# The beginning of an RWKV-7 scan: the last columns of v between its first products, and the first inverse ahead of the second pair's scores

## The chip, the cores and the metric

The kernel runs on one core of one Trainium2 chip. The metric is the device time of one execution in microseconds. The time before is the median of three runs, 1482.53 us (1478.01 to 1484.24). One further execution was profiled; it took 1480.0 us, and its trace has a span of 1478.1 us. All instants below are microseconds from the start of that span. Engines are named as the profile does: PE is TensorE, DVE VectorE, ACT ScalarE, POOL GpSimd, SP SyncE (here it only issues transfers).

## The reference

Two layers over 1024 tokens of width 1024, each with a norm before and a residual add after, and a last norm. The first layer (chunked gMLP beside dilated attention) is not touched. The second is RWKV-7 time mixing. Its inputs are shifted mixes of the normed activations, its projections r, k, v and a gate g, and its core is a recurrence per head with a 64x64 state:

```python
xr, xw, xk, xv, xa, xg = [h + xx * mu[i] for i in range(6)]
r, k, v, g = xr @ w_r, xk @ w_k, xv @ w_v, xg @ w_g
...
def step(state, inp):
    r_t, w_t, k_t, v_t, kk_t, a_t = inp
    sa = jnp.einsum('bhvk,bhk->bhv', state, -kk_t)
    state = (state * w_t[:, :, None, :]
             + sa[..., None] * (kk_t * a_t)[:, :, None, :]
             + v_t[..., None] * k_t[:, :, None, :])
    y_t = jnp.einsum('bhvk,bhk->bhv', state, r_t)
    return state, y_t
...
y = (y + bonus) * jax.nn.silu(g)
return y @ w_o
```

## The kernel before, in words

**The scan.** The 1024 tokens are cut into 16 chunks of 64, for 16 heads. Inside a chunk the recurrence is a triangular system per head: with M, the strictly triangular products of the chunk's scaled keys (`A`, `BK`), the chunk needs X, the inverse of a unit triangular matrix built from M. Chunks are handled in pairs (b2); eight pairs in all. For one pair the work is:

- `ld`: SyncE loads `A` and `BK` (0.5 MB each) of a chunk from DRAM, where the projections left them (L1001, L1003).
- `al` (alphas): 64 small matmuls (L1043, L1046) into two PSUM banks; ScalarE copies them to `M` (L1047) and `AK` (L1048).
- `sM`, `lM`: M goes to DRAM in four stores (L1055) and comes back, in another layout, as `Nt` (L1099, two loads).
- `ip`: GpSimd clears the inverse's tiles. `ia`, `ie`, `ib` (8 pieces): the inverse itself, on VectorE alone (L1121 to L1164).
- `ic`, `lX`: the result goes to DRAM as `XT` (L1171) and comes back as `X` (L1179).
- `mx`, `ma`, `mb`: the merge, two small groups of matmuls (L1197, L1210) with a copy by ScalarE after each (L1200, L1213).
- `sc` (half of a chunk's scores, 32 matmuls, L1030, one PSUM bank, copied by ScalarE to `MY`), `mA`, `mY` (triangular masks, GpSimd), `dec` (BK times the decay, GpSimd, L1062), `T` (transposes of BK, L1072).
- Then the serial part per chunk: `V` (L1225), `W` (L1235), `U` (L1250), `st` (the state, L1275, added by VectorE, L1277), `Y`.

**The gate.** 16 column blocks of the gate's projection (first eight for tokens 0 to 511, then eight for 512 to 1023) are TensorE's filler between these small products. A piece `g1` is three matmuls of 128x512 (L943); eight pieces make a block, which ScalarE passes through SiLU (L949). Block n needs its weight: `L` loads it (SyncE, L928, 0.5 MB), `wx` splits it into a high part (ScalarE, L105) and a low part (L106; GpSimd for n from 2 to 7, VectorE for the others). `xl` loads the gate's operands of the second half of the tokens into the tiles of the first half (L937, 1 MB each). 64 pieces stand in the beginning.

**What sets the order.** Up to the scan a scheduler places the instructions. In the scan each engine, SyncE's queue too, runs its instructions in the order in which the code calls them. That order is three strings of such names with a number each: `SCAN_START`, `SCAN_STEP` (six times), `SCAN_END`. An instruction whose input is not there holds up all that stands behind it on its engine. Matmuls of the gate and of `V`, `W`, `U`, `st` share three PSUM banks, `al`, `T`, `ma` and `mb` two others, which are given out in turn.

**v.** The projection of v is made in four chunks of 256 columns, each for eight blocks of 128 tokens: 24 matmuls of 128x256 (L153) for a block and chunk, since every operand is split into a high and a low part and three of the four products are taken. Two blocks fill a PSUM bank; ScalarE copies it out (L855) and SyncE stores it (L857). After the first half of the last chunk the operands of the gate are made (`mixed`: L736, L739 on ScalarE, L737 and L740 on VectorE, L740 on GpSimd too), then the second half follows. All of v is done before `SCAN_START` begins.

Of the kernel before, what the change touches and what calls it, by code (L numbers as in the profile page):

```python
# [8 lines left out]
F32 = mybir.dt.float32  # L9
# [8 lines left out]
P = 128  # L18
KT = D // P
NB = S // P  # L20
CB = 256
# [28 lines left out]
EVEN_PLAN = (  # L50
    "q0 k0 h0 z2 h1 q1 h2 k1 h3 va0 s0 h4 u0 h5 z3 h6 z0 h7 va1 s1 u1 z1")
SCAN_START = (
# [4 lines left out]
SCAN_STEP = (  # L57
    "U0 al0 ib2 st0 al1 Y0 uv1 keep1 mA0 mA1 W1 sM0 sc0 ib3 ld6 U1 sc1 g1 mY0 mY1 ic0 st1 dec0 lM0 Y1 g1 W2 keep2 "
    "ip0 lX0 gx1 uv2 sc2 Yd0 T0 g1 sc3 ia0 ld7 mx0 ma0 dec1 ie0 g2 mb0 g2 T1 g2 ib3 gl2")
# [771 lines left out]
            nc.sync.dma_start(g.BK_d[64:128, f * 8:(f + 1) * 8, p, 1 - j], BK[64:128, :, j])  # L831


def odd_layer(g, a, hT, wt, out):
    nc, tc = g.nc, g.tc
    st = ExitStack()
# [13 lines left out]

    def ev_v(c):
        def fn(b2, ps):
            t = g.s2([P, 2, 2, CB // 2], F32, "rt")
            for j in range(2):
                nc.scalar.activation(t[:, j].rearrange("p e (q d) -> p e q d", d=CH),  # L855
                                     ps[:, j].rearrange("p (q e d) -> p e q d", e=2, d=CH), AF.Copy)
                nc.sync.dma_start(g.v_d[(2 * b2 + j) * P:(2 * b2 + j + 1) * P, :, c * P:(c + 1) * P], t[:, j])  # L857
        return fn
# [6 lines left out]
    w = load_wm(g, plan[0][1], 0)  # L865
# [4 lines left out]
    for j, (i, W, fn, ld, ev, c) in enumerate(plan):  # L870
        if c == 0:
            x, xn = xn, ({}, {})
        if j + 1 < len(plan):
            nxt = plan[j + 1][3](g, plan[j + 1][1], plan[j + 1][5] * CB)
        else:
            gate = Gate(g, a["rw_wg"][0], xn)
            gate.load(0)
            gate.load(1)
            gate.split(0)
            gate.split(1)  # L880
        if j == 9:
            norms(g)
        if j == XD:
            mixed_out(g, hT, 5, 1, g.xg_d)
        if c == 3:
            ni = plan[j + 1][0] if j + 1 < len(plan) else 5
            fn(g, x, w, ev(c), (0,))
            mixed(g, hT, ni, (0,), xn)
            fn(g, x, w, ev(c), (1,))
            if ni != 5:  # L890
                mixed(g, hT, ni, (1,), xn)
        else:
            fn(g, x, w, ev(c))
        w = nxt
# [83 lines left out]
class Rwkv:  # L978
# [326 lines left out]
    def start(self, gate):  # L1305
        g, nc = self.g, self.g.nc

        def zs(i):
            nc.gpsimd.memset(self.new_S(0), 0.0)

        self.pm = g.bB([P, 2, 2, 4, CH], "pm")
        ops = dict(L=gate.load, wx=gate.split, xl=gate.load_x, ld=self.load,
                   g=lambda i: [next(gate.rest, None) for _ in range(i)],
                   sc=lambda i: self.scores(i // 2, i % 2), al=self.alphas, sM=self.store_M, lM=self.load_M,
                   ip=self.inverse_p, ia=self.inverse_a, ie=self.inverse_d, ib=lambda i: [next(self.rows, None) for _ in range(i)],
                   ic=self.inverse_c, lX=self.load_X, mx=self.merge_x, ma=self.merge_a, mb=self.merge_b,
                   dec=self.decayed, T=self.transposed, mA=self.mask_AK, mY=self.mask_MY,
                   uv=self.load_uv, V=lambda i: list(self.Wkeys(i)), W=self.W, keep=self.keep, zs=zs)
        for name, i in order(SCAN_START):
            ops[name](i)  # L1320
# [244 lines left out]
```

## Time and profile before

| | us |
|---|---|
| median of three runs | 1482.53 (1478.01 to 1484.24) |
| profiled execution, its own time | 1480.0 |
| its span | 1478.1 |
| TensorE busy | 1308.3 (89%) |
| VectorE busy | 897.8 (61%) |
| ScalarE busy | 627.8 (42%) |
| GpSimd busy | 548.4 (37%) |
| last matmul of v ends, about | 1003.1 |
| first inverse on VectorE | 1038.1 to 1069.2 |
| first merge product (L1197), all but two of it | 1078.3 |
| first `U` (L1250) | 1089.0 |

Matmuls are pipelined, so a busy TensorE is not TensorE at its peak: 87 matmuls of v begin in 10 us, though each is shown as lasting 0.28 us. In the chain of waits a row gives start, duration and what ran; "SPq" is the time in which SyncE issues a transfer, "DMA a<-b" the time from the end of the issue to the transfer's end. In rows by stretch the columns are the stretch, its length, busy time (and instructions) of PE, weight loads, DVE, ACT and POOL, then the granted TensorE clock, the share of the DMA engines and GB/s. In rows by group the two numbers after the bar are busy us and mean ns of one, and behind the second bar stands the idle time before them and what ended it.

### The profile page before, as it was taken

Reading aid. Unit: us, or ns where it says so; the run is one execution under the profiler, and the core shown is the slowest. Engines: PE = TensorE matmul, PEld = TensorE weight load, DVE = VectorE, ACT = ScalarE, POOL = GpSimd, SP = SyncE. Lnnn points to the kernel's source line nnn. Section 1 sums busy time; section 2 is a strip of 40 time slices with the busy share of each in tenths; the row PEclk is TensorE's granted clock in tenths of the full one; section 3 lists DMA queues with packets and bytes.
Section 4 is the critical chain, followed back from the end, with each engine's and each line's share of the span. In section 5 each row is a group of like instructions: output and inputs, shape, how many; then the busy total and the mean of one; then the engine's idle time right before and its main releaser. Section 6 shows DMA issues by size and latency. Waiting matters only on the chain.

```text
span 1478.1 us, 30910 instructions
## 1 busy us (share of the span) xinstructions
PE 1308.3 (89%) x12773; PEld 1108.9 (75%) x12773; DVE 897.8 (61%) x1489; ACT 627.8 (42%) x1188; POOL 548.4 (37%) x353
## 2 busy tenths in 40 slices
PE   5899999899997999999997868998978788887877
PEld 5887788778896799978864436896767666667877
DVE  8741535663557426771599888512856677768884
ACT  4421535552454323552545554323434344454322
POOL 8750102030112612221343353203644444387751
PEclk9999999899999999999999979998978898979998
DMA  6377435350443334224177547517586666676412
GB/s 221 86 259 196 114 128 158 83 131 15 137 121 101 124 119 143 74 74 140 43 220 203 125 103 204 143 48 207 142 244 162 154 168 167 187 212 228 143 36 93
DMA packets 253275, 209.15 MB, mean 141 GB/s; under 512 B 79648, under 2 KB 215424, under 8 KB 253136
## 3 DMA queue, kind: packets, MB, share of 16 engines
q1 hardware_dynamic: 249536, 198.27, 47.1%
q10 hardware_dynamic: 3600, 8.91, 1.8%
q8 instruction: 100, 1.64, 0.5%
q14 instruction: 39, 0.32, 0.1%
HBM read 135.71 MB, written 71.43 MB: 140 GB/s over the span
## 4 chain that ended last, share of the span: by engine, by line
PE 53%; DVE 17%; DMA 9%; issue 8%; ACT 6%; POOL 4%; SPq 2%; ACTq 0%; DVEq 0%; POOLq 0%
PE pj L153 33%; PE pj L943 4%; PE pt L572 2%; PE pj L1477 2%; DMA kl<-dk 1%; DMA BK<-BK_d 1%; DMA w<-in_rw_a_dram 1%; DMA XT<-xm 1%; PE sp L562 1%; PE sp L559 1%; PE op L580 1%; DMA X<-XT 1%; ACT wh L105 1%; PE py L1285 1%; DVE xm L737 1%
## 5 line engine op out<-in xcount | busy, mean ns | idle before, releaser
L106 POOL TENSOR_TENSOR wl<-wraw,wh 128x1024 fp32r<-128x1024 f32 x38 | 93.6, 2466 | 168.6 <-ACT wh L105 157.5
L106 DVE TENSOR_TENSOR wl<-wraw,wh 128x1024 fp32r<-128x1024 f32 x46 | 70.8, 1545 | 94.5 <-ACT wh L105 51.4
L153 PE MATMUL pj<-hh,wh 128*128 128x512 f32 x320 | 127.3, 398 | 0.0
L153 PE MATMUL pj<-hh,wl 128*128 128x512 f32 x320 | 126.6, 396 | 0.0
L153 PE MATMUL pj<-hl,wh 128*128 128x512 f32 x320 | 126.6, 396 | 0.0
L105 ACT ACTIVATE wh<-wraw 128x1024 fp32r<-128x1024 f32 x84 | 88.1, 1056 | 61.9 <-DMA wraw<-in_w_in_even_dram 25.1
L153 PE MATMUL pj<-xl,wh 128*128 128x512 f32 x256 | 102.3, 400 | 2.6 <-DVE xl L740 2.6
L153 PE MATMUL pj<-xh,wh 128*128 128x512 f32 x256 | 102.2, 401 | 2.4 <-ACT ks L789 2.4
L153 PE MATMUL pj<-xh,wl 128*128 128x512 f32 x256 | 101.8, 398 | 0.2 <-POOL wl L106 0.2
L566 DVE CUSTOM_DVE_ANT_0 sc<-sp,tb 128x128 f32<-128x128 f32 (+3 forms) x64 | 48.2, 753 | 59.4 <-PE sp L562 50.8
L1477 PE MATMUL pj<-wh,yh 128*128 128x256 f32 x256 | 75.4, 294 | 5.1 <-DVE x L1481 3.9
L1477 PE MATMUL pj<-wh,yl 128*128 128x256 f32 x256 | 74.4, 291 | 4.6 <-POOL yl L106 4.5
L153 PE MATMUL pj<-wh,hh 128*128 128x256 f32 x256 | 75.1, 296 | 3.2 <-ACT hh L265 2.9
L737 DVE SCALAR_TENSOR_TENSOR xm<-hT,pr,xm 128x512 f32<-128x512 f32 x56 | 50.0, 933 | 44.0 <-ACT xm L736 43.7
L153 PE MATMUL pj<-wh,hl 128*128 128x256 f32 x256 | 75.3, 295 | 1.2 <-DVE hl L266 1.2
L153 PE MATMUL pj<-wh,yl 128*128 128x256 f32 x256 | 73.7, 288 | 1.9 <-POOL yl L624 1.9
L153 PE MATMUL pj<-wl,hh 128*128 128x256 f32 x256 | 74.6, 292 | 0.0
L153 PE MATMUL pj<-wh,yh 128*128 128x256 f32 x256 | 73.3, 286 | 0.8 <-ACT yh L623 0.8
L1477 PE MATMUL pj<-wl,yh 128*128 128x256 f32 x256 | 74.0, 289 | 0.0
L153 PE MATMUL pj<-wl,yh 128*128 128x256 f32 x256 | 72.9, 285 | 0.0
L153 PE MATMUL pj<-wh,xh 128*128 128x256 f32 x256 | 72.2, 282 | 0.6 <-ACT ks L789 0.5
L153 PE MATMUL pj<-wl,xh 128*128 128x256 f32 x256 | 72.2, 282 | 0.0
(320 smaller groups left out, 4062.3 us busy)
## 6 DMA issues: line engine op xcount, KB each, us to landing
wraw<-in_w_in_even_dram SPq DMA_DIRECT2D x28, 512.0 KB
tb<-tb SPq DMA_DIRECT2D x16, 512.0 KB
A_d<-AR SPq DMA_DIRECT2D x16, 512.0 KB
wraw<-in_rw_wg_dram SPq DMA_DIRECT2D x16, 512.0 KB
A<-A_d SPq DMA_DIRECT2D x16, 512.0 KB
BK<-BK_d SPq DMA_DIRECT2D x16, 512.0 KB
xt<-in_x_dram SPq DMA_DIRECT2D x8, 512.0 KB
dv<-vt SPq DMA_DIRECT2D x16, 256.0 KB
```

The costliest lines, as they stand in the source:

```text
L105: nc.scalar.activation(hi, raw, AF.Copy)
L106: sub.tensor_tensor(lo, raw, hi.bitcast(F32), OP.subtract)
L153: nc.tensor.matmul(ps, a(k), b(k), start=(n == 0), stop=(n == 3 * KT - 1))
L559: nc.tensor.matmul(sp[:, c0:c1], qs[:, b * P:(b + 1) * P], kh[:, c0:c1], start=True, stop=False)
L562: nc.tensor.matmul(sp[:, c0:c1], qs[:, b * P:(b + 1) * P], kl[:, c0:c1], start=False, stop=True)
L566: nc.vector.tensor_tensor_reduce(sc[:, :n], sp[:, :n], tb[:, off:off + n], 1.0, BIG, OP.add, OP.min, mn)
L572: nc.tensor.transpose(pt[:, j - j0, :], sc[:, j * P:(j + 1) * P], g.ident)
L580: nc.tensor.matmul(op[:, s0:QW], vt[:, j, :], pth[j // 4][:, j % 4, s0:QW], start=(j == 0), stop=False)
L737: nc.vector.scalar_tensor_tensor(t, hT[kk, f][:, j, 0:512], g.pr[:, i, k:k + 1], t, op0=OP.mult, op1=OP.add)
L943: nc.tensor.matmul(ps, u[:, k], v[:, k % 2], start=(k == 0 and i == 0), stop=(k == KT - 1 and i == 2))
L1285: nc.tensor.matmul(self.py[64 - 64 * e:128 - 64 * e, q], t["MY"][:, 8 * e + q], t["UV"][:, e, q], start=q == 0, stop=False)
L1477: nc.tensor.matmul(ps[:, i, :], u[:, k], v[:, k % 4], start=(k == 0 and j == 0), stop=(k == KT - 1 and j == 2))
```

## The change

The second half of v's last chunk is no longer made before the scan. It becomes a generator of eight steps of 12 matmuls each (half a block of 128 tokens), which a new name in the string, `vp`, advances: three before the first `al`, one between the two, four after the second. Its output tile is named `XT` instead of `rt`. The string `SCAN_START` is rewritten; it holds the same names and 64 pieces of the gate as before, and `vp` beside them. `SCAN_STEP` and `SCAN_END` are unchanged.

```diff
 SCAN_START = (
-    "g4 L2 g4 L4 L3 g7 al0 al1 sM0 ip0 wx2 g2 sc0 L7 g2 sc1 dec0 L9 uv0 ld2 g3 wx3 sc2 g2 wx4 sc3 dec1 g2 lM0 T0 "
-    "ld3 L6 g4 mA0 mY0 ia0 L5 g2 al2 wx5 g2 sc4 T1 ld4 g3 al3 sM1 ie0 sc5 dec2 g3 wx6 ib8 sc6 g2 sc7 dec3 uv1 T2 "
-    "zs0 g3 ic0 g4 wx7 mA1 mY1 ip1 lM1 lX0 keep0 g4 T3 g5 L8 mx0 xl0 V0 uv2 ma0 g2 wx8 xl1 ia1 mA2 g2 xl2 mb0 ie1 "
-    "W0 ld5 mA3 g2 xl3 ib3")
+    "vp3 al0 vp1 al1 sM0 ip0 vp2 lM0 vp2 ia0 ie0 g4 L2 sc0 g4 L4 L3 sc1 dec0 ib8 ld2 g7 wx2 g2 sc2 L7 g2 sc3 dec1 "
+    "L9 uv0 T0 ld3 g3 wx3 ic0 ip1 lX0 g2 wx4 T1 al2 mA0 mY0 g2 L6 ld4 g4 sc4 L5 g2 wx5 mx0 al3 sM1 V0 uv2 ma0 sc5 "
+    "dec2 g2 mb0 T2 g3 lM1 sc6 g3 wx6 sc7 dec3 ia1 mA1 mY1 uv1 g2 zs0 g3 ie1 T3 g4 wx7 keep0 g4 mA2 g5 L8 xl0 g2 "
+    "wx8 xl1 g2 xl2 W0 ld5 mA3 g2 xl3 ib3")
...
+def last_values(g, x, w, evac):
+
+    wh, wl = w
+    for b in range(4, 8):
+        sl = slice((b % 4) * P, (b % 4 + 1) * P)
+        if b % 2 == 0:
+            ps = g.bA([P, 2, CB], "pj")
+        n = 0
+        for k in range(KT):
+            for i, v in ((0, wh), (0, wl), (1, wh)):
+                g.nc.tensor.matmul(ps[:, b % 2, :], x[i][k // 2, 1][:, k % 2, sl], v(k), start=(n == 0), stop=(n == 3 * KT - 1))
+                n += 1
+            if k == 3:
+                yield
+        if b % 2:
+            evac(b // 2, ps)
+        yield
...
     def ev_v(c):
         def fn(b2, ps):
-            t = g.s2([P, 2, 2, CB // 2], F32, "rt")
+            t = g.s2([P, 512], F32, "XT").rearrange("p (j e c) -> p j e c", j=2, e=2)
...
             mixed(g, hT, ni, (0,), xn)
-            fn(g, x, w, ev(c), (1,))
             if ni != 5:
+                fn(g, x, w, ev(c), (1,))
                 mixed(g, hT, ni, (1,), xn)
+            else:
+                gate.last = last_values(g, x, w, ev(c))
...
-        ops = dict(L=gate.load, wx=gate.split, xl=gate.load_x, ld=self.load,
+        ops = dict(vp=lambda i: [next(gate.last, None) for _ in range(i)], L=gate.load, wx=gate.split, xl=gate.load_x, ld=self.load,
```

Two places where the order moves are of use later. In the new kernel the same statements have line numbers higher by up to 21, and instances of a tile carry other numbers. The first is SyncE's queue at the scan's first loads. `A_9328` and `A_9332` are the first two chunks' A before, `BK_9330` and `BK_9334` their BK, `wraw` a weight of the gate. Before:

```order
L857 DMA v_d_126<-rt_9260 256x1x128 x2
L1001 DMA A_9328<-A_d_116 128x1024
L1001 DMA A_9332<-A_d_116 128x1024
L928 DMA wraw_9352<-in_rw_wg_dram 128x8x128
L857 DMA v_d_126<-rt_9314 256x1x128 x2
L928 DMA wraw_9369<-in_rw_wg_dram 128x8x128
L928 DMA wraw_9371<-in_rw_wg_dram 128x8x128
L1003 DMA BK_9330<-BK_d_117 128x1024
L1003 DMA BK_9334<-BK_d_117 128x1024
L1055 DMA MA_0_129<-M_9395 32x16x32 x4
```

And now:

```order
L876 DMA v_d_126<-XT_9158 256x1x128 x2
L1022 DMA A_9220<-A_d_116 128x1024
L1022 DMA A_9224<-A_d_116 128x1024
L1024 DMA BK_9222<-BK_d_117 128x1024
L1024 DMA BK_9226<-BK_d_117 128x1024
L876 DMA v_d_126<-XT_9318 256x1x128 x2
L1076 DMA MA_0_129<-M_9268 32x16x32 x4
L1120 DMA Nt_9393<-MA_0_129 64x1024 x2
L876 DMA v_d_126<-XT_9420 256x1x128 x2
```

BK follows A at once, and `Nt` follows the stores of M; the loads of weights, UV and the next chunks come after them.

The second is the first X, on SyncE and on ScalarE, now. On SyncE, `wraw_9752` and `wraw_9788` are the weights that `L6` and `L5` load, `A_9754` and `BK_9756` belong to the fifth chunk, `MA_1` is the second pair's M:

```order
L1192 DMA XT_0_137<-xm_9363 1024x1x32 x2
L1200 DMA X_9216<-XT_0_137 32x16x32 x4
L949 DMA wraw_9752<-in_rw_wg_dram 128x8x128
L1022 DMA A_9754<-A_d_116 128x1024
L1024 DMA BK_9756<-BK_d_117 128x1024
L949 DMA wraw_9788<-in_rw_wg_dram 128x8x128
L1076 DMA MA_1_130<-M_9703 32x16x32 x4
```

Before, those two weights and that chunk were loaded ahead of `XT_0`, and M of the second pair was stored ahead of it too; they now stand behind the X loads. On ScalarE, `wh_9799` is the high part of `wraw_9788`, `M_9703<-pt_9805` the second pair's last M copy, `rt_9866` and `X_9216` the merge's two copies:

```order
L970 ACTIVATE XT_9796<-pj_9745 128x512
L971 DMA sg_d_115<-XT_9796 128x512
L105 ACTIVATE wh_9799<-wraw_9788 128x1024
L1068 ACTIVATE M_9703<-pt_9805 128x512
L1069 ACTIVATE AK_9704<-pt_9806 128x512
L1221 ACTIVATE rt_9866<-pt_9865 32x512 x2
L1052 ACTIVATE MY_9770<-pm_9230 128x2x256
L1234 ACTIVATE X_9216<-pt_9926 32x16x32 x2
```

Before, the merge's copies followed a SiLU and its store, and that M copy stood 16 rows ahead of them.

## The prediction

> **What bounds the kernel now.** I read the page first, then the chain of waits around the place of the edit, then the table of who TensorE waits for, and last the single rows of SyncE, ScalarE, VectorE and GpSimd there. The edit sits between the last product of v and the first `U` (L1250), in this execution about 992 to 1089 us.
>
> ```profile
> span 1478.1 us, 30910 instructions
> ```
>
> The chain of waits there (start, duration, what):
>
> ```profile
> 1003.14 5.58 PE pj L943 x24
> ...
> 1009.33 6.83 DMA BK<-BK_d
> ...
> 1018.09 0.61 ACT M L1047
> ...
> 1021.07 0.61 ACT M L1047
> 1021.69 0.33 SPq L1055
> ...
> 1023.13 0.52 SPq L1055
> ...
> 1029.05 9.04 DMA Nt<-MA
> 1038.11 1.66 DVE DN L1121
> ...
> 1068.22 0.96 DVE xm L1164
> 1070.11 3.05 DMA XT<-xm
> ...
> 1074.59 3.63 DMA X<-XT
> 1078.27 1.91 PE pt L1197 x62
> ...
> 1086.58 8.21 DMA BK<-BK_d
> ```
>
> So the end hangs on one serial line: v's products, the loads of BK, the copies of M, M through DRAM to `Nt`, the inverse on VectorE (1038.1 to 1069.2, 31.1 us), its result through DRAM to `X`, then TensorE to the first `U`:
>
> ```profile
> 1088.96 0.27 PE L1250 MATMUL ch<-Ws,X 64*64 64x64 f32 x2
> ```
>
> TensorE's own waits in that stretch (total, times, longest), the two large ones, are small beside the 97 us:
>
> ```profile
> PE pt L1197 <- DMA X<-XT: 8.1, 2, 6.3
> PE pt L1043 <- DMA BK<-BK_d: 2.6, 1, 2.6
> ```
>
> 10.7 us of waits on transfers, in 97 us of which nearly all else is work. Both kinds of work that the edit moves, matmuls of v and pieces of the gate, are TensorE's, and their number is unchanged. So the edit can earn only what it takes out of such waits, and the half clock that follows one (busy by engine, then PEclk):
>
> ```profile
> 970.00:980.00 10.00, 10.00 (x87) 10.00 (x86) 0.00 (x0) 0.66 (x2) 0.00 (x0) 1.00 0.19 52
> 1016.20:1023.00 6.80, 5.89 (x131) 4.58 (x131) 0.00 (x0) 3.02 (x6) 0.00 (x0) 0.51 0.10 26
> 1078.20:1084.70 6.50, 6.43 (x73) 5.40 (x74) 1.94 (x5) 2.23 (x3) 0.00 (x0) 0.50 0.88 274
> 1074.00:1084.00 10.00, 6.01 (x73) 5.07 (x74) 2.12 (x3) 2.23 (x3) 3.95 (x7) 0.52 0.88 239
> ```
>
> **The change, part by part.** I rebuild the line in instants of this execution and compare the first `U`, 1088.96. Nothing is added but order: the tile renamed from `rt` to `XT` costs nothing, since the copies and stores of v are the same and each is read out while TensorE works on the next pair.
>
> *The moved matmuls.* 96 of v's matmuls leave the place ahead of the scan. At 87 in 10 us they are 11.0 us, so the first half of v ends at 1003.1 - 11.0 = 992.1. In this execution SyncE and ScalarE then show:
>
> ```profile
> 1005.03 1.21 SPq L857 DMA_DIRECT2D v_d<-rt  x2
> 1009.33 2.00 SPq L1003 DMA_DIRECT2D BK<-BK_d  x2
> 1004.10 0.63 ACT L739 ACTIVATE xh<-xm 128x512 fp32r<-128x512 f32 x1 [2.16 <-DVE xm L737]
> ```
>
> The loads of BK no longer stand behind three loads of gate weights. After the first half's last two stores of v (1.2 us) and two loads of A (as much) they go at about 994.6 instead of 1009.3, and with the 6.83 us of the chain's row land at 1001.4. But the copy of the first M stands on ScalarE behind the gate's operands, whose last one ends at 1004.73. That, not BK, is what is late next: of 14.7 us won on the load, 13.4 are left (first M copy 1004.7 instead of 1018.1). From there to the end of the second M copy it took 3.6 us; 1008.3.
>
> *M through DRAM.* Before, `Nt` stood behind two weights, a UV and a pair of A and BK; now it follows M's stores. Four stores take 2.0 us (1021.69 to 1023.65); their landing is not shown apart, the nearest row is XT's, 3.05 us; two issues 1.1; and the flight with little ahead of it is seen one step later:
>
> ```profile
> 1107.42 2.81 SPq L1099 DMA_DIRECT2D Nt<-MA  x2
> 1114.34 0.53 DVE L1121 TENSOR_TENSOR DN<-Nt,rn 128x256 f32<-128x256 f32 x1 [1.74 <-DMA Nt<-MA]
> ```
>
> 1114.34 - 1110.23 = 4.1. Together 10.2 (bounds: 8, if M's quarter-size stores land in half of XT's time, and the 16.4 of before). The inverse starts at 1018.5, 19.6 us early.
>
> *The inverse.* Its length depends on GpSimd. The first inverse met seven long two-input operations there, the second inverse none of them, and took 19.8 us, of which 0.7 is the state's addition:
>
> ```profile
> 1083.73 0.42 DVE L1121 TENSOR_TENSOR DN<-Nt,rn 128x256 f32<-128x256 f32 x1
> 1102.60 0.95 DVE L1164 TENSOR_REDUCE xm<-tm 128x96 f32<-128x768 f32 x1
> ```
>
> By groups, in 1038 to 1069.2 and then 1083.7 to 1103.6:
>
> ```profile
> L106 POOL TENSOR_TENSOR wl<-wraw,wh 128x1024 fp32r<-128x1024 f32 x4 | 9.6, 2398 | 9.7 <-ACT wh L105 9.7
> L1062 POOL TENSOR_TENSOR BK<-BK,EC 128x1024 f32<-128x1024 f32 x3 | 6.5, 2157 | 0.9 <-PE pm L1030 0.9
> L1131 DVE TENSOR_TENSOR tm<-DN 128x4 f32<-128x4 f32 (+6 forms) x7 | 5.1, 731 | 0.3
> L1159 DVE TENSOR_REDUCE R<-tm 128x36 f32<-128x864 f32 (+3 forms) x5 | 4.5, 902 | 0.2
> ...
> L1159 DVE TENSOR_REDUCE R<-tm 128x36 f32<-128x864 f32 (+3 forms) x5 | 4.5, 901 | 0.2
> L1131 DVE TENSOR_TENSOR tm<-DN 128x4 f32<-128x4 f32 (+6 forms) x7 | 1.7, 243 | 0.3
> ```
>
> The same seven small products cost 731 ns each beside GpSimd and 243 alone; the reductions are alike. 31.1 - 19.1 = 12.0 over seven operations is 1.7 each. In the new order the two decays of BK and two splits of gate weights fall into the inverse; the third split stands behind a memset that waits for the inverse's own store. Four times 1.7 is 6.8: 25.9 us, end at 1044.4 (bounds: 19.1 and 31.1). The Trainium skill (SBUF — State Buffer, "Who interferes with whom") calls the port pair of the two engines an exclusive lock, which two-input VectorE operations meet and reductions on trn2 never do. The trace agrees (731 against 243, 902 against 901); by that rule a collision can cost as much as the operation's rest, at most 9.1 us for these four, and the sum below would be up to 2.3 higher.
>
> *X and what stands beside it.* XT from the inverse's end (1069.18) to its landing (1073.16) took 4.0: 1048.4. The X loads landed 5.1 later: 1053.5. Here a new wait comes in. On ScalarE the split of the gate weight that is loaded last (`L5`) now stands ahead of the second pair's last M copy and of the merge's copies, and the first merge matmul (L1197) needs the bank that this M copy frees. That weight's load stands on SyncE behind the X loads, another weight, A and BK, and so behind XT's landing. Bytes from the first X load: four loads of 0.52 MB and 0.26 of X are 2.36 MB; at the 239 GB/s of the row for 1074 to 1084, a stretch with the same kind of loads, 9.9 us: 1058.3. Its split:
>
> ```profile
> 1081.44 1.06 ACT L105 ACTIVATE wh<-wraw 128x1024 fp32r<-128x1024 f32 x1
> ```
>
> 1.06 and 0.6 for the M copy: the merge starts at 1060.0, not at 1053.5. (Cheapest: the weight is there with X, and only `V0` behind its mask, 1.1 us of memsets, one split 2.4 and one mask 1.4 after XT, and its own 1.2, stands ahead: 1054.5.) TensorE has nothing else queued: its list up to there (half of v's moved matmuls, 5.5; 32 gate pieces at 5.58 / 8 = 0.70, 22.3; and about 8 of small products) is out at about 1045, counted from 1008.
>
> *The tail.* From the first merge to `U` before: 1088.96 - 1078.27 = 10.7, with six gate pieces. Now 32 pieces stand there, and three half-scores and two transposes of the second pair:
>
> ```profile
> L1030 PE MATMUL pm<-A,BK 64*64 64x64 f32 x256 | 5.8, 230 | 0.4 <-ACT MY L1031 0.4
> L1072 PE MATMUL pt<-ident,BK 128*128 128x128 f32 x32 | 4.3, 276 | 0.0
> ```
>
> 26 x 0.70 = 18.2, 3 x 0.72 = 2.2, 2 x 1.07 = 2.1: 33.2 in all. The last transpose waits for GpSimd's split and decay (0.6 + 1.06 + 2.4 + 2.2 after a gate copy) with 4.2 us of matmuls as cover: 2 more. `U` at 1095.2, **6.2 us late**. The half clock after the wait is inside the 10.7: the row for 1078.2 to 1084.7 shows 6.5 us at 0.50, and the new wait is no shorter. The Trainium skill (TensorE: Matmul & The Clock Gate, "The HAM clock gate") releases the clock after about 3.4 us of sustained work. This trace shows nearly twice that; with the page's figure the new tail would be an estimated 1.6 us shorter (half of 6.5 - 3.4), and the sum below 6.4.
>
> *The step behind.* BK for the second product of step 0 now queues behind three loads of gate operands (1.05 MB each) given out within 3 us, where the first went out 10 us before the others:
>
> ```profile
> 1075.80 0.67 SPq L937 DMA_DIRECT2D xh<-xg  x1
> 1083.07 0.33 SPq L937 DMA_DIRECT2D xh<-xg  x1
> ```
>
> TensorE already waited there, until 1094.9. One more MB at the 327 GB/s of 1083 to 1095 is 3.2 us, plus 0.5 for the later start: 0 to 3.7, I take 1.9.
>
> ```profile
> 1083.00:1095.00 12.00, 9.55 (x273) 7.84 (x274) 11.10 (x28) 4.64 (x8) 0.00 (x0) 0.93 0.92 327
> ```
>
> Sum: 6.2 + 1.9 = **8 us slower**, against the profiled execution's own 1480.0 us (1478.1 and 1.9 around it): 1488. The median of the three runs shown is 1482.5, 2.5 higher; the runs spread by 6.2, and I don't add it.
>
> **The rivals.**
> *The cover works.* Inverse as short as the second one (GpSimd's work falls beside it), M's landing 2 us shorter, the gate weight there in time: start 1016.5, end 1035.6, X at 1044.7, merge 1045.9, tail 33.2: `U` at 1079.1, 9.9 early; with the step's wait between 0 and 1.9: 1470 to 1472. For it: the bare inverse is in the trace. Against: the two decays must run before the transposes, which TensorE wants in that very time. It decides once the weight lands within 2 us of X and at most one long GpSimd operation falls into the inverse.
> *The wait only moves.* As forecast, but the gate weight lands with X: merge 1054.5, tail 35.2, `U` 1089.7, and 1.9: 1483. For it: the transfers fill 16 engines, and order of landing is not order of issue to the microsecond. Against: nothing else is in flight that it could overtake but the three loads ahead of it.
> *The inverse collides as before.* 31.1 us, for the masks and splits come where TensorE's list lets them: 5.2 later than forecast, 1493. It decides from the fifth long GpSimd operation on.
> *It doesn't do what it says:* if the M copy were not ready until the gate's operands and more were done, the 19.6 us of head start would shrink; each microsecond there is one on the end. It is in the range.
>
> **How the numbers follow.** Forecast 0.40, wait only moves 0.25, cover works 0.20, collides as before 0.15. The range 1472 to 1496 leaves out the best part of the cover's case and what lies beyond the collision; the forecast's own is 1482 to 1493. What can be told from no change is 0.5%, 7.4 us around 1482.5, so 1475 to 1490. Slower: all of 0.15 and somewhat over half of the forecast's 0.40, 0.38; faster: most of the 0.20, 0.16; the rest 0.46.
>
> **What would show it.** BK landing near 1001 and the first M copy near 1004.7; `Nt` about 20 us earlier; the first inverse 24 to 28 us; TensorE idle for over 10 us ahead of the first merge, with its end set by the split of a gate weight on ScalarE; the first `U` later than 1089; a longer wait for BK in step 0. I am wrong if the merge starts with X's landing, if the inverse takes about 20 us, or if the tail holds less than 30 us.

## The result, and the profile after

The changed kernel is slower. Over seven runs each, its median is 1490.8 us (1489.4 to 1498.7) against 1478.9 (1474.7 to 1484.2) for the kernel before: ratio 1.010, 95% interval 1.007 to 1.013, some 15 us (the two medians alone differ by 11.9). Beside the experiments it was run again: ratio 1.012 (1.009 to 1.015). The prediction said 1488, between 1472 and 1496, as 8 us on top of 1480. The sign and the mechanism came out; the 8 us are about half of what the ratios give. That 1490.8 still lies so near 1488 is in part luck: the seven runs of the kernel before have a median of 1478.9 and not the 1482.5 of the first three. The size is worth taking apart, for over a quarter of what the traces lose lies where the prediction never looked.

The profiled execution took 1498.7 us, the slowest of its seven, so both it and a second profiled execution (1492.9) are used below. The page of the first:

```profile
span 1496.6 us, 30917 instructions
```

The chain of waits around the place of the edit (start, duration, what), where before the load of X stood ahead of the merge:

```profile
995.05 5.72 DMA BK<-BK_d
...
1007.44 0.61 ACT M L1068
...
1010.37 1.96 DMA MA<-M
...
1013.03 3.83 DMA Nt<-MA
...
1043.74 4.34 DMA XT<-xm
...
1051.85 7.62 DMA wraw<-in_rw_wg_dram
1059.56 1.06 ACT wh L105
1060.62 0.49 ACT M L1068
1061.16 1.92 PE pt L1218 x64
...
1077.69 2.38 POOL wl L106
1080.08 1.88 POOL BK L1083
1082.00 1.97 PE pt L1093 x8
1083.97 12.46 PE pj L964 x51
...
1097.92 10.97 DMA BK<-BK_d
1109.03 0.37 PE pt L1064 x2
```

The transfer that ends last ahead of the merge is no longer X but `wraw`, a weight of the gate, and behind it stand its split (`wh`) and the copy of M, both on ScalarE. TensorE's table of waits in 985 to 1125 us (total, times, longest) has grown from two large rows to four:

```profile
PE pt L1064 <- DMA BK<-BK_d: 10.1, 2, 5.6
PE ch L1246 <- POOL AK L1099: 6.3, 1, 6.3
PE pt L1218 <- ACT M L1068: 6.2, 1, 6.2
PE pt L1093 <- POOL BK L1083: 2.2, 1, 2.2
```

Executions differ by up to 7 us in what lies ahead of the scan, so instants are compared from the end of the last matmul (L153) of v's first half. In the kernel before that is 991.8, the end of the 97th matmul of v from the last, 0.1 us ahead of ScalarE's copy of that half; the prediction had estimated 992.1. Its instants are counted from 991.8 too. In us from there:

| | before | predicted | changed | changed, again |
|---|---|---|---|---|
| first M copy begins | 26.3 | 12.9 | 12.8 | 12.8 |
| second M copy ends | 29.9 | 16.5 | 15.9 | 15.6 |
| inverse begins (VectorE) | 46.3 | 26.7 | 24.8 | 25.2 |
| inverse ends | 77.4 | 52.6 | 50.9 | 49.8 |
| first merge product | 84.4 | 68.2 | 69.0 | 67.3 |
| first `U` | 97.2 | 103.4 | 106.8 | 104.9 |
| step 0, first product of `Y` | 106.0 | 114.1 | 118.8 | 117.3 |
| first merge product of the next pair | 123.1 | | 136.4 | 135.1 |
| end of the span | 486.3 | 494.3 | 504.4 | 503.0 |

So 8 to 10 us are lost by the first `U`, 11 to 13 by step 0's `Y`, and 17 to 18 by the end. TensorE's side of the first of these, from the end of v's first half to the first `U` (length, busy time and instructions of PE, weight loads, VectorE, ScalarE, GpSimd, then its clock, the share of the DMA engines, GB/s), before and after:

```profile
991.80:1089.00 97.20, 83.30 (x1028) 67.54 (x1027) 48.47 (x67) 39.41 (x66) 44.40 (x36) 0.89 0.65 183
```

```profile
992.20:1099.00 106.80, 84.53 (x1024) 69.47 (x1023) 46.78 (x71) 39.83 (x66) 42.71 (x36) 0.87 0.53 153
```

The same work in both; idle time grew from 13.9 to 22.3 us, and the rest of the difference, 1.2 us, goes with the lower clock. TensorE, not any chain, is what one should count here, and the experiments bear that out.

### The profile page after: what moved, and what is told of

The parts are those of the page before. It is cut to its first block, busy times and chain, and to the rows that moved or that the text cites. A ratio compares the mean times of both kernels' runs of the same rounds, so it can differ in the third digit from the quotient of the medians.

```text
span 1496.6 us, 30917 instructions
## 1 busy us (share of the span) xinstructions
PE 1304.2 (87%) x12773; PEld 1105.5 (74%) x12773; DVE 890.1 (59%) x1489; ACT 628.4 (42%) x1188; POOL 548.1 (37%) x353
## 4 chain that ended last, share of the span: by engine, by line
PE 54%; DVE 14%; DMA 10%; issue 8%; ACT 6%; POOL 6%; SPq 2%; ACTq 0%; DVEq 0%; POOLq 0%
PE pj L153 32%; PE pj L964 4%; PE pt L572 2%; PE pj L1498 2%; PE pj L711 1%; DMA BK<-BK_d 1%; DMA XT<-xm 1%; PE op L580 1%; PE sp L559 1%; DMA X<-XT 1%; PE sp L562 1%; POOL wl L106 1%; ACT wh L105 1%; DVE xm L737 1%; PE ch L1296 1%
## 5 line engine op out<-in xcount | busy, mean ns | idle before, releaser
L153 PE MATMUL pj<-hh,wh 128*128 128x512 f32 x320 | 127.3, 398 | 0.0
L153 PE MATMUL pj<-hl,wh 128*128 128x512 f32 x320 | 126.7, 396 | 0.0
L153 PE MATMUL pj<-hh,wl 128*128 128x512 f32 x320 | 126.7, 396 | 0.0
L153 PE MATMUL pj<-xh,wh 128*128 128x512 f32 x256 | 103.0, 404 | 2.5 <-ACT ks L789 2.4
L153 PE MATMUL pj<-xl,wh 128*128 128x512 f32 x256 | 102.9, 403 | 2.6 <-DVE xl L740 2.6
L153 PE MATMUL pj<-xh,wl 128*128 128x512 f32 x256 | 102.5, 400 | 0.5 <-POOL wl L106 0.5
L153 PE MATMUL pj<-wh,hh 128*128 128x256 f32 x256 | 74.7, 295 | 2.9 <-ACT hh L265 2.6
L153 PE MATMUL pj<-wh,hl 128*128 128x256 f32 x256 | 74.9, 293 | 1.2 <-DVE hl L266 1.2
L153 PE MATMUL pj<-wh,yl 128*128 128x256 f32 x256 | 73.7, 288 | 1.9 <-POOL yl L624 1.9
L153 PE MATMUL pj<-wl,hh 128*128 128x256 f32 x256 | 74.3, 291 | 0.0
L153 PE MATMUL pj<-wh,yh 128*128 128x256 f32 x256 | 73.3, 286 | 0.9 <-ACT yh L623 0.9
L153 PE MATMUL pj<-wl,yh 128*128 128x256 f32 x256 | 72.8, 285 | 0.0
L575 DVE TENSOR_TENSOR ptl<-pt,pth 128x512 fp32r<-128x512 f32 (+2 forms) x96 | 52.4, 553 | 29.9 <-ACT pth L574 16.8
L153 PEld LDWEIGHTS pj<-hh,wl 128*128 128x128 f32 x320 | 60.1, 188 | 13.3
```

What stands on the lines that cost most here:

```text
L153: nc.tensor.matmul(ps, a(k), b(k), start=(n == 0), stop=(n == 3 * KT - 1))
L575: nc.vector.tensor_tensor(ptl[j0 // 4][:, 0:j1 - j0, i * P:(i + 1) * P], pt[:, :j1 - j0, :], o.bitcast(F32), OP.subtract)
```

## The experiments

Ratios are to the kernel before, run beside on the same chip. Unless something else is said, each is the changed kernel with its string `SCAN_START` edited; the diffs show the names of the string that move.

### The weight's place on SyncE

```diff
-... T0 ld3 g3 wx3 ic0 ... g2 L6 ld4 g4 sc4 L5 g2 wx5 ...
+... T0 ld3 L6 L5 g3 wx3 ic0 ... g2 ld4 g4 sc4 g2 wx5 ...
```

> The loads of the gate weights L6 and L5 stand on SyncE ahead of XT's store instead of behind the X loads; nothing else moves. Theory (the weight that lands at 1059.5 holds ScalarE, and with it the second pair's M copy and the merge): ScalarE's 13.3 us wait is gone, the merge starts behind V0 at about 1054.9 instead of 1061.2, the first U at about 1092.8 instead of 1099.0, and the time is 6 us less, 1484 to 1485. Rival (the weight's wait lies beside another wait that ends as late, such as X or the masks): the merge starts within 1 us of 1061 and the time stays at 1490 to 1491. Second rival (two more loads ahead of XT delay X): X lands later than 1051 and the time is 1491 or more.

Measured: 1481.8 us, ratio 1.002 (0.999 to 1.004). On ScalarE and TensorE of this run:

```profile
1044.19 1.06 ACT L105 ACTIVATE wh<-wraw 128x1024 fp32r<-128x1024 f32 x1 [0.40 <-ACT XT L970]
1045.16 0.58 ACT L1068 ACTIVATE M<-pt 128x512 f32<-128x512 f32 x1
...
1047.15 1.23 PE L1246 MATMUL ch<-UV,AK 64*64 64x64 f32 x32 [2.90 <-POOL AK L1099]
1048.30 1.92 PE L1218 MATMUL pt<-X,M 32*32 32x32 f32 x64
```

The split no longer waits, and the merge begins 1.2 us behind `V0`. That is 59.2 us from the end of v's first half instead of 67.3 to 69.0, and the first `U` stands at 95.4 instead of 104.9 to 106.8: 9.5 to 11.4 us, 3 to 5 more than expected. Some 1.5 of this lie between the merge and `U` (36.2 us against 37.7 and 37.8), with less half clock (mean clock from the end of v's first half to the first `U` 0.93 against 0.87). The rest is that the merge itself comes 3.5 us earlier than the expected 62.7, for `V0` waited only 2.9 us for its mask in this execution.

### The split's place on ScalarE

```diff
-... g2 wx5 mx0 al3 sM1 V0 uv2 ma0 sc5 dec2 g2 mb0 T2 ...
+... g2 mx0 al3 sM1 V0 uv2 ma0 sc5 dec2 g2 mb0 wx5 T2 ...
```

> The loads stay where they are; only the split of the weight that L5 loads (wx5) moves behind the merge (mb0), since block 5 of the gate is not asked for until 40 pieces are done. Theory (it is ScalarE's order, not the transfer itself, that costs): as with the early loads, merge at about 1054.9, first U at about 1093, 1484 to 1485. Rival (the transfer takes bandwidth or queue places from X and BK, and so moving the split gains less): gain under 2 us, 1489 to 1491, while the run with the early loads gains.

Measured: 1483.0 us, ratio 1.002 (0.999 to 1.004), the same as with the early loads; merge at 62.4, `U` at 98.7. On TensorE:

```profile
1052.06 1.97 PE L1246 MATMUL ch<-UV,AK 64*64 64x64 f32 x32 [6.28 <-POOL AK L1099]
1053.96 1.27 PE L1218 MATMUL pt<-X,M 32*32 32x32 f32 x39
```

The weight's transfer stays as late as it was, and nothing else is moved but one activation and its subtraction: what costs is that ScalarE works in order and stood behind a weight that nobody needed yet. Against the changed kernel's profile the merge is 6.6 us earlier and `U` 8.1, close to the 6.2 that TensorE waited; the 3.3 us by which `U` is later than with the early loads are mostly `V0`'s longer wait for its mask in this execution (6.28 against 2.90 us). In the changed kernel itself the two profiled executions differ there by as much (`V0` at 60.8 and 58.3). By the ratios the run gains 12 to 15 us, more than these 6 to 8; another 5.3 us come behind the next pair's merge, to which the last experiment returns.

### The place of `ld5` on SyncE

`ld5` loads the chunk whose BK TensorE waits for in step 0. Counted from `ld0` it is the sixth; the expectations call it the fifth.

```diff
-... g5 L8 xl0 g2 wx8 xl1 g2 xl2 W0 ld5 mA3 ...
+... g5 ld5 L8 xl0 g2 wx8 xl1 g2 xl2 W0 mA3 ...
```

> The load of the fifth chunk's A and BK (ld5) moves ahead of the weight L8 and the three pairs of loads of the gate's operands; nothing else moves. Theory (BK's 11.0 us landing behind those loads is the second part of the loss): TensorE's 5.6 us wait for BK in step 0 is gone, the first U stays at 1099, the time is 5 to 6 us less, 1485. By the prediction's own bound for that term the gain is at most 3.7 plus the 2.4 that TensorE waited there before. Rival (the operands then land later and TensorE waits for them in the first pieces of block 8 instead): gain under 2 us, 1489 to 1491.

Measured: 1482.9 us, ratio 1.001 (0.999 to 1.004). From the first `U` to `Y` step 0 takes 8.1 us where the changed kernel takes 12.0 and 12.4: the 5.6 us wait for BK is gone (2.6 us remain, which the profile puts down to issue) and 4 us are won, within the bound. But the end is 12 to 13 us earlier, and the ratio says as much. The last experiment explains a part of the rest.

### v first

```diff
-vp3 al0 vp1 al1 sM0 ip0 vp2 lM0 vp2 ia0 ie0 ...
+vp8 al0 al1 sM0 ip0 lM0 ia0 ie0 ...
```

> All eight steps of v's deferred matmuls stand ahead of the first alphas (vp8 al0 al1 ...), the rest of the new order is as in the change: the new order without v between the first products. Theory (the first M copy waits for the gate's operands on ScalarE, which end at about 1005, so v between the products buys nothing): TensorE loses its 4.5 us wait for BK, the second M copy ends at 1005 to 1007 instead of 1008.05, the inverse starts 1 to 3 us earlier, and the time is 1 to 3 us less, 1488 to 1490. Rival (v between the products brings M forward, as its place suggests): M copies 3 to 5 us later, inverse later by as much, 1494 to 1496.

Measured: 1494.8 us, ratio 1.010 (1.007 to 1.014), as slow as the changed kernel. The theory missed and the rival half hit: the first M copy starts at 16.6 instead of 12.8, the inverse at 28.5. The cause is on ScalarE again. All of v's copies now stand ahead of M's, and the second pair of them waits, by the profile, 2.6 us for a store of v:

```profile
1008.33 0.66 ACT L874 ACTIVATE XT<-pj 128x256 f32<-128x256 f32 x2 [2.62 <-DMA v_d<-XT]
1008.87 0.60 ACT L1068 ACTIVATE M<-pt 128x512 f32<-128x512 f32 x1
```

TensorE waits 4.9 us for that copy of M where it waited 4.5 for BK. The delay shrinks on its way: the inverse, which met GpSimd at other moments, took 24.0 us, the merge came at 69.7, and the first `U` at 105.6 lies between the two executions of the changed kernel.

### Early M in the old order

The string of before stands behind an early M; only the second half of the new order is undone.

```diff
-... ia0 ie0 g4 L2 sc0 g4 L4 L3 sc1 dec0 ib8 ld2 g7 ... (the new order)
+... ia0 ie0 ib8 g4 L2 g4 L4 L3 g7 wx2 g2 sc0 ... (the order of before, without al0 al1 sM0 ip0 lM0 ia0 ie0 ib8)
```

> One part of the change alone: v's last columns stand between the first products, M's stores and loads (sM0, lM0) and the first inverse follow at once, and behind them stands the string of before in its old order, with the second pair's scores and 58 pieces of the gate ahead of the merge. Theory (the early M was worth having, and the loss comes from the new order behind it, where the merge stands ahead of TensorE's filler and waits): X is there long before TensorE has done its 58 pieces, the 8.1 us of waits for X that before had are gone with the half clock behind them, BK's wait ahead of the first products grows from 2.6 to 4.5; first U 8 to 10 us earlier than before's relative to the end of v's first half, ratio to before 0.993 to 0.995 (1471 to 1474). Rival (the early M itself costs, through BK's wait and half clock at the beginning): ratio 1.000 or more.

Measured: 1470.5 us, ratio 0.994 (0.992 to 0.996): as the theory had it, faster than both kernels. From the end of v's first half to the first `U`:

```profile
986.70:1071.20 84.50, 78.12 (x1024) 64.04 (x1023) 40.23 (x59) 39.48 (x66) 46.21 (x36) 0.98 0.74 205
```

Idle time is 6.4 us, 4.4 of it the wait for BK at the beginning, and the clock is 0.98. X is taken over at 68.8, but the merge runs at 76.6, because TensorE has work until then. So the early M is worth 9 us by the ratio and 12.7 at `U`, and the new order behind it takes all that back and more: at `U` it is 20 to 22 us behind this one.

### The same with `ld5` early

```diff
-... g5 L8 mx0 xl0 V0 ... W0 ld5 mA3 ...
+... g5 ld5 L8 mx0 xl0 V0 ... W0 mA3 ...
```

> As the run with the old order behind an early M, and the load of the fifth chunk (ld5) stands ahead of the weight L8 and the gate's operands. Theory: TensorE's wait for BK in step 0 (2.4 us in before) goes too: 2 to 3 us less than the run with the old order, ratio 0.991 to 0.994. Rival: the operands of the gate land later and TensorE waits for them: no difference between the two.

Measured: 1469.3 us, ratio 0.993 (0.991 to 0.995). It cannot be told from the run before it, so the expected 2 to 3 us are not shown; both beat the changed kernel and the kernel before. The wait for BK in step 0 is replaced by one of 2.9 us that the profile puts down to issue, and `Y` comes 9.5 us behind `U` instead of 9.8.

### Both mends together

```diff
-... T0 ld3 g3 ... L6 ld4 ... sc4 L5 g2 ... g5 L8 xl0 ... W0 ld5 mA3 ...
+... T0 ld3 L6 L5 g3 ... ld4 ... sc4 g2 ... g5 ld5 L8 xl0 ... W0 mA3 ...
```

> The changed kernel with both mends together: L6 and L5 ahead of XT's store, ld5 ahead of L8 and the gate's operands. Theory (two separate losses, 11.4 us at the first U and 5.3 us at BK in step 0): they add up, 16 to 17 us less than the changed kernel, ratio to before 0.995 to 0.998 (1474 to 1478). Rival (one is hidden behind the other): no faster than each of them alone, ratio 1.001 to 1.002.

Measured: 1477.8 us, ratio 0.999 (0.997 to 1.001). Against 1.010 to 1.012 this is 16 to 20 us: the sum expected, though the interval also holds the rival's 1.001. In the trace they add: `U` at 95.6 as with the early weight, `Y` 8.2 behind it as with the early `ld5`. What each mend alone had won in later pairs does not add: by their ratios each is worth 12 to 16 us. What is left against the run with the old order is 11 us at `U`: idle 13.8 us against 6.4, clock 0.93 against 0.98. The idle time is made of BK's 4.8 and of small waits, none above 2.3 us, at the second pair's scores, products and transposes and at `V0`. These stand between TensorE's filler in another rhythm than in the old order, and neither of the two mends touches them.

### What GpSimd does to the inverse

Left out are the low parts of the gate weights of blocks 2 and 3, so this is a lighter computation.

```diff
-            self.w[n] = split(self.g, self.raw.pop(n), [P, KT, P], "w", ...)
+            nc.scalar.activation(hi, raw, AF.Copy)          # n = 2, 3
+            nc.gpsimd.memset(lo.bitcast(F32), 0.0)
```

> The changed kernel, in which the low parts of two gate weights (blocks 2 and 3) are left out: GpSimd clears the tile instead of subtracting, so two of the four long two-input operations inside the first inverse are gone. Theory (1.7 us of the inverse for each): the inverse takes 26.2 - 3.4 = 22.8 us, XT's store, the weight that loads behind it, the merge and the first U come 3.4 us earlier, 1487. Rival (the inverse's length doesn't depend on these, but on the decays or the masks): it stays at 26 and the time at 1490 to 1491. Third possibility: it shrinks by up to 4.8 (two operations of 2.4 us, each of which shuts VectorE out for all of its time).

Measured: 1489.7 us, ratio 1.007 (1.005 to 1.010); the inverse takes 21.0 us instead of 26.2 and 24.6, `U` is at 99.8, 5 to 7 us earlier. That is 3.6 to 5.2 us off the inverse: at the least the theory's 3.4, at the most a little over the third possibility. The rows tell why. In the changed kernel, GpSimd:

```profile
1020.50 1.91 POOL L1083 TENSOR_TENSOR BK<-BK,EC 128x1024 f32<-128x1024 f32 x1 [14.36 <-PE pm L1051]
1023.82 2.42 POOL L106 TENSOR_TENSOR wl<-wraw,wh 128x1024 fp32r<-128x1024 f32 x1 [1.40 <-ACT wh L105]
1030.34 1.92 POOL L1083 TENSOR_TENSOR BK<-BK,EC 128x1024 f32<-128x1024 f32 x1 [4.10 <-PE pm L1051]
1032.96 2.40 POOL L106 TENSOR_TENSOR wl<-wraw,wh 128x1024 fp32r<-128x1024 f32 x1 [0.71 <-ACT wh L105]
```

and VectorE in the same stretch:

```profile
1020.55 2.08 DVE L1152 TENSOR_TENSOR tm<-DN 128x196 f32<-128x196 f32 x1
1023.89 2.63 DVE L1178 TENSOR_TENSOR tm<-Nt,xm 128x256 f32<-128x256 f32 x1
...
1030.44 2.37 DVE L1183 TENSOR_TENSOR tm<-DN,R 128x512 f32<-128x512 f32 x1
1032.84 0.69 DVE L1185 TENSOR_REDUCE xm<-tm 128x64 f32<-128x512 f32 x1
1033.56 2.72 DVE L1178 TENSOR_TENSOR tm<-Nt,xm 128x864 f32<-128x864 f32 x1
```

In the lighter run the same four shapes took 0.36, 0.42, 0.69 and 1.06 us, with no two-input operation of GpSimd running when they started. The excess is 1.7, 2.2, 1.7 and 1.7: 7.3 us, and 26.2 - 7.3 = 18.9 is the bare inverse. Each of the four products starts while a two-input operation of GpSimd runs and ends 0.2 to 0.9 us after that operation's end. The reduction at 1032.84 ran beside one and took the 0.69 us that it also took in the lighter run. There the two decays that were left cost 1.6 and 0.5, and 21.0 - 2.1 is the same 18.9: GpSimd's two clears of 0.95 us cost nothing. The changed kernel's second execution gives it a third time: four operations there cost 1.75, 2.10, 0.88 and 0.98, and 24.6 - 5.7 = 18.9. One of its four is not a product but a pair of copies (2.56 us against 0.46). The Trainium skill (SBUF — State Buffer, "Who interferes with whom") calls the ports that the two engines share an exclusive lock: whoever issues first has them for the whole instruction, and the other fully blocks. These rows agree. So what one operation costs is its rest at the moment of collision, 0.5 (the lighter run's second decay) to 2.2 us, and not a constant.

### Six steps of v ahead of the first products

On the old order with `ld5` early:

```diff
-vp3 al0 vp1 al1 sM0 ip0 vp2 lM0 vp2 ia0 ...
+vp6 al0 al1 sM0 ip0 vp2 lM0 ia0 ...
```

> The run with the old order behind an early M and the early fifth chunk, with six of v's eight steps ahead of the first alphas and two behind M's stores (vp6 al0 al1 sM0 ip0 vp2 lM0): six steps are 8.3 us of matmuls, about the 8.5 us after which BK lands, and the first M copy waits for the gate's operands until 12.8 us anyway. Theory (behind the old order TensorE's own work sets the end, so what it idles at the beginning counts in full): the 4.4 us wait for BK and the half clock behind it (1.6 us) go, M comes no later, the first U is 5 to 6 us earlier, ratio to before 0.989 to 0.990 (1462 to 1464 at 1478). Rival (M comes later and holds the inverse, or the clock falls somewhere else): no gain, 0.993.

Measured: 1464.8 us, ratio 0.994 (0.991 to 0.996): no gain that can be told, though its median is the lowest of all. TensorE's wait changed its name and hardly its length:

```profile
994.80 0.27 PE L1064 MATMUL pt<-BK,A 64*64 64x64 f32 x2 [1.41 <-DMA BK<-BK_d]
998.84 0.48 PE L1064 MATMUL pt<-BK,A 64*64 64x64 f32 x4 [2.88 <-ACT M L1068]
```

1.41 + 2.88 = 4.3 where it was 4.9 in the run that this one is edited from: the second `al` needs the banks that the first M copy empties, and that copy waits on ScalarE for the gate's operands, as the prediction had said. The place of v between the first products is therefore no worse than this one; it fills the second wait instead of the first.

The same edit on the changed kernel with both mends:

```diff
-vp3 al0 vp1 al1 sM0 ip0 vp2 lM0 vp2 ia0 ... L6 L5 ... ld5 L8 ...
+vp6 al0 al1 sM0 ip0 vp2 lM0 ia0 ... L6 L5 ... ld5 L8 ...
```

> The changed kernel with both mends (L6, L5 and ld5 early) and the same six steps of v ahead of the first alphas. Theory (in the new order the merge stands ahead of the filler and waits for X, so time won by TensorE ahead of it is given back there): the wait for BK goes, but TensorE waits longer for the masks and X at V0 and the merge; first U at most 2 us earlier than 95.6 us after v's first half, ratio to before 0.997 to 0.999. Rival (TensorE's work sets the end here too): 5 to 6 us earlier, ratio 0.995.

Measured: 1480.0 us, ratio 1.003 (1.000 to 1.005), `U` at 96.3, no earlier. That `U` gains nothing agrees with the theory, the ratio does not: it lies above the 0.997 to 0.999 expected. And since the edit gained nothing in the other order either, it tells the two apart no longer.

### The changed kernel once more

> The changed kernel itself once more, beside the others. Its profiled execution took 1498.7 us where the median of its runs is 1490.8, so one execution more shows which of its waits repeat. Theory: those at BK (4.5), V0 (6.3), the merge (6.2), GpSimd's decay (2.2) and BK in step 0 (5.6) repeat within 1 us, and ScalarE's 8.3 us at a store of the gate near 1304 does not; ratio to before 1.007 to 1.012. Rival: the wait near 1304 repeats and is a cost of the change.

Measured: 1493.5 us, ratio 1.012 (1.009 to 1.015). BK's two waits (10.2 us in all), the merge's (7.9 after 6.2) and the decay's (2.2) come again; `V0`'s 6.3 us do not, they are 1.2 here. `V0` and the merge together waited 9.1 us instead of 12.5. And the store's wait on ScalarE near 1300 us, taken for an accident, repeats. Here:

```profile
1297.13 0.60 ACT L1052 ACTIVATE MY<-pm 128x512 f32<-128x512 f32 x1 [10.06 <-DMA lnw<-in_rw_lnw_dram]
```

and in the first profiled execution:

```profile
1303.70 0.33 ACTq L971 DMA_DIRECT2D sg_d<-XT  x1
1304.08 0.60 ACT L1052 ACTIVATE MY<-pm 128x512 f32<-128x512 f32 x1 [8.25 <-DMA lnw<-in_rw_lnw_dram]
```

### The store 300 us behind the edit

In the built program every transfer counts on one of eight semaphores, and one that shares a semaphore waits for the earlier transfer on it. The store of the gate (L971) in question waited for a store of Y in the kernel before:

```profile
1283.95 0.60 ACT L1031 ACTIVATE MY<-pm 128x512 f32<-128x512 f32 x1 [2.97 <-DMA Y<-Y]
```

In the changed kernel, whose transfers come in another order, its partner is the load of `lnw`, which lands later. Nothing of that is written in the change.

```diff
-"Lr1 S0 Fl0 U0 ib2 g1 Fm0 Lr5 ...        (the string of the scan's end)
+"Fl0 U0 ib2 g1 Fm0 Lr1 S0 Lr5 ...
```

> The changed kernel, in which two names at the head of the last string (Lr1, the load of an output weight, and S0, the loads of lnw and of the bonus) stand behind Fm0 instead. In the built program each transfer counts on one of eight semaphores, and the store of the gate on ScalarE near 1304 us waits for an earlier transfer on its own: for a store of Y in the kernel before, in the run with ld5 early and in the run with both mends, for the load of lnw in the changed kernel and in the others; here it is a store of Y again. Theory (that wait is part of the change's cost, though its place is 300 us behind the edit): ScalarE's wait there falls from 8.3 and 10.1 us to 3 to 5.5, TensorE's behind it from 7.2 and 7.7 to 1 to 4, and the time is 4 to 5 us less, ratio to before 1.007 to 1.009 where the changed kernel has 1.010 to 1.012. Rival (another wait ends as late): no difference, 1.010 to 1.012.

Measured: 1487.3 us, ratio 1.006 (1.004 to 1.007).

```profile
1292.92 0.38 ACTq L971 DMA_DIRECT2D sg_d<-XT  x1
1293.35 0.60 ACT L1052 ACTIVATE MY<-pm 128x512 f32<-128x512 f32 x1 [2.98 <-DMA Y<-Y]
```

ScalarE's wait is 3.0 us as before the change, TensorE's behind it 1.6 instead of 7.2 and 7.7, and from the next pair's first merge to the end the kernel takes 361.0 us instead of 368.0 and 367.9; before it was 363.2. By the ratios it is 7 to 10 us, somewhat more than the 4 to 5 expected; the interval touches the first one of the changed kernel and lies below the second. The partner holds over all the traces: with Y's store (before, the early `ld5`, both mends, this one) the wait is 3.0, 3.7, 5.5 and 3.0 us, with `lnw` in the ten others 7.8 to 10.1. The moved loads also leave the DMA engines freer at that moment, and this run does not part the two.

What the partner is worth can be read from all 14 traces, if the time behind the edit is cut in two, so that the store stands in the second stretch. In us:

| | next pair's merge to the sixth pair's | from there to the end | the store waits for |
|---|---|---|---|
| before | 134.0 | 229.2 | Y |
| changed | 134.8 | 233.2 | `lnw` |
| changed, again | 131.4 | 236.5 | `lnw` |
| split later on ScalarE | 129.2 | 233.5 | `lnw` |
| `ld5` early | 130.4 | 230.8 | Y |
| both mends | 134.6 | 232.7 | Y |
| this run | 130.4 | 230.6 | Y |

The second stretch takes 229.2 to 232.7 us in the four traces with Y's store and 233.2 to 236.5 in the ten with `lnw`, in the mean 230.8 and 233.9. In three of the four the moved loads stand in their old place, so it is the partner that parts the two groups, and it is worth about 3 us. The first stretch takes 127.6 to 135.6 us in the 14, the longer the lower its clock (0.99 to 0.89), whatever the partner; why the clock differs there is open. Of the 7 us that this run's trace gains behind the next pair's merge, 1.0 to 4.4 lie in that stretch and are not shown to be the store's. It is the same with the early `ld5`; and the later split, with `lnw`, is 5.6 us shorter than the changed kernel's first execution in the first stretch and 0.2 longer in the second.

## Why the prediction was right in sign and too small

**BK early and the first M copy: right.** The issue was predicted at 994.6 and seen at 995.05; BK landed at 1000.8 (1001.4); the first M copy began at 1004.96 (1004.7), held by the gate's operands and not by BK, as said. (Its 11.0 us for the moved matmuls were 11.3 in the kernel before: 1003.1 - 991.8.) The run with six steps of v shows the same bound from the other side.

**M through DRAM: right within its bounds, a little long.** 8.9 and 9.6 us from the second M copy's end to the inverse against 10.2, because the four stores landed in 1.96 us and not in XT's 3.05.

**The inverse: right, 26.2 (and 24.6) against 25.9.** Exactly the four predicted operations of GpSimd fell into it, in both executions. The constant of 1.7 each was a fair mean of what was 0.5 to 2.2 in these rows.

**The new wait ahead of the merge: right, and shown.** The weight landed at 1059.5 (1058.3), the merge began at 1061.16 (1060.0), set by a split on ScalarE. Two runs that remove this wait in two ways, one on SyncE and one on ScalarE, win back 9 to 11 and 6 to 8 us at `U` and bring the ratio to 1.002.

**The tail: the term that was sized too small.** Between merge and `U` the prediction put 35.2 us; it took 37.8 and 37.6. The waits in it were 2.9 and 2.4 us where 2 were taken. The rest is half clock: the sum had the 6.5 us of the kernel before, and the two executions had 10.1 and 11.2. The first, from the merge on, in four stretches:

```profile
1061.20:1067.90 6.70, 6.70 (x138) 5.48 (x140) 0.00 (x0) 2.16 (x4) 3.81 (x2) 0.50 0.56 118
1067.90:1082.00 14.10, 11.21 (x141) 8.46 (x137) 4.64 (x18) 5.11 (x8) 4.31 (x3) 0.98 0.26 68
1082.00:1085.40 3.40, 3.40 (x13) 3.06 (x14) 0.00 (x0) 1.19 (x2) 3.25 (x4) 0.53 0.40 117
1085.40:1099.00 13.60, 13.60 (x86) 10.64 (x84) 4.43 (x6) 3.92 (x5) 6.75 (x8) 1.00 0.39 129
```

The first is the known one, 6.7 us here against 6.5 before. The third follows TensorE's wait of 2.2 us for GpSimd's decay: 3.4 us at 0.53, which costs 1.6. The second execution, from the merge to that wait's end and for 3.4 us behind it, and then the run with the loads behind `Fm0`, whose order is the same up to there, behind its merge:

```profile
1055.10:1066.30 11.20, 10.96 (x178) 8.99 (x179) 1.60 (x8) 4.52 (x8) 3.81 (x2) 0.50 0.57 121
1066.30:1077.20 10.90, 8.72 (x95) 6.36 (x93) 3.07 (x11) 2.74 (x4) 4.30 (x3) 1.00 0.10 35
1077.20:1080.60 3.40, 3.38 (x19) 2.94 (x20) 0.00 (x0) 1.25 (x3) 3.25 (x4) 1.00 0.42 123
1060.30:1066.50 6.20, 6.18 (x118) 4.96 (x120) 0.00 (x0) 2.23 (x4) 3.88 (x2) 0.50 0.52 99
```

Here the same 2.2 us wait brings no half clock, but the half clock behind the merge lasts 11.2 us; in the last run it lasts 6.2, and that tail took 36.1 us, near the forecast. So the size that was missed differs between executions of one order, and the decay's wait is not shown to cost more than its length each time. The Trainium skill (TensorE: Matmul & The Clock Gate, "The HAM clock gate") gives about 3.4 us for the release; the third stretch of the first execution agrees with it, the first, behind a longer wait and with products of 32x32 in it, took twice as long in both kernels, and in the second execution three times.

**BK in step 0: the other undersized term.** Taken at 1.9 of 0 to 3.7; from `U` to `Y` step 0 takes 3.2 and 3.6 us longer than before, the upper end. BK landed 10.97 us after its issue, behind six operands of 0.5 MB given out in the 4.3 us ahead of it. The run with that load ahead of them won 4.

**The step that failed: that nothing else is moved.** The sum ended at step 0. It treated the rest of the program as fixed since its strings are unchanged. But the transfers' semaphores are given out over the whole program, and the new order gave one store on ScalarE a later partner. From the next pair's merge to the end the changed kernel takes 4.8 us longer than before in both traces, and the run that gives the store its old kind of partner has them back. About 3 us of this go with the partner in all the traces; what the remainder is stays open.

With these the first trace has 9.6 us at `U`, 3.2 in step 0 and 4.8 behind, 17.6, and the second 7.7, 3.6 and 4.8, 16.1. The traces show 18.1 and 16.7 (the rest lies between `Y` and the next pair's merge), the ratios 15 to 18, the forecast 6.2, 1.9 and nothing.

**The rivals.** "The cover works" fell: TensorE was idle for 12.5 us around `V0` and the merge (9.1 in the second execution, just under the 10 that the prediction named as a sign). "The wait only moves" fell with the weight's landing, 7.6 us behind its issue and 8.5 us after VectorE had taken X over (1051.0). "The inverse collides as before" fell with four operations instead of seven. What none of them said is that the early M alone, without the rest of the new order, is worth 9 us.

## What to carry to other kernels

Count TensorE's idle time and half clock over the whole stretch, and ask of a new order not which chain it shortens but what TensorE does while that chain runs: the same early start won 9 us with the old order behind it and ended 15 to 18 us behind with the new. On an engine that works in order, a load that nobody needs yet is as harmful as one that is late, as soon as something urgent stands behind its consumer. And after any change in the order of transfers, compare the waits to the end of the program and not only around the edit.

## What was not expected of the hardware

- The wait of 2.2 to 2.4 us for GpSimd's decay was followed by half clock, 3.4 us of it, in three of the ten traces that have it (the changed kernel, `ld5` early, both mends), and by full clock in seven. Ahead of the merge a wait of 6.2 us was followed by 6.7 us of work at half clock, though `V0` had run for 2 us at half clock just before, and one of 7.9 us by 11.2.
- In the changed kernel's trace the clock is at half from 999.8 to 1006.7, 1051.0 to 1068.1, 1081.8 to 1085.2 and 1105.7 to 1112.5: 6.8, 17.1, 3.4 and 6.8 us, each a whole multiple of 3.4. Of the 371 such stretches of these 14 traces all but 12 are, so in this kernel half clock is best counted in steps of 3.4 us.
- VectorE's two-input products, and once a pair of copies, wait out GpSimd's two-input operations, 0.5 to 2.2 us each; GpSimd's clears of the same tile (0.95 us) and VectorE's reductions show nothing of it.
- Six loads of 0.5 MB and A given out within 4.3 us ahead of BK stretch its landing to 10.97 us; without them ahead of it at the scan's beginning it took 5.72.
- Open: why TensorE's wait of 2.9 us remains in step 0 when BK is early, which the profile puts down to issue.
